# A two-layer hybrid decoder: sums of the experts back to the tokens in converted passes, one gathering product for 256 slots, another order of the parts, a later residual

## The chip, the cores and the metric

One core of a Trainium2 chip runs the whole kernel. The metric is the device time of one execution in microseconds; the time before is the median of three runs. TensorE multiplies, VectorE (DVE) and ScalarE (ACT) do the elementwise work and read the products out of PSUM, SyncE (SP) issues the weight loads, GpSimd (POOL) does little.

## The reference, cut to what matters

Two layers on 256 tokens of 1024 channels. Each has a token mixer and a channel mixer, with a layer norm behind each. The channel mixer of layer 0 is one dense SwiGLU, that of layer 1 is the part that the change touches:

```python
def moe_ffn(h, w_router, w13, w2):               # 256 tokens, 8 experts, top 2
    logits = (t @ w_router).astype(jnp.float32)
    top_v, top_i = lax.top_k(logits, TOP_K)
    probs = jax.nn.softmax(top_v, axis=-1)
    gates = (jax.nn.one_hot(top_i, N_EXPERTS) * probs[..., None]).sum(-2)
    for e in range(N_EXPERTS):
        out = out + gates[:, e, None] * swiglu(t, w13[e], w2[e])
...
x = layer_norm(ALPHA * x + (1 + g_f) * y, ln_g[l, 1], ln_b[l, 1])
```

Everything is float32, and each expert has 3584 hidden channels, so that its three matrices are 42 loads of 1 MB.

## The kernel before

**Two kinds of product.** A float32 product leaves two records in the trace and is slow. The kernel avoids it where much work goes over the same weights: `convert` (L120) rounds a half megabyte of weights to a short form, `hi` (ACT, L123), and takes the rest, `lo` (DVE, L125), and `passes` (L496) makes three fast products of `hi` and `lo` of both factors. `split` (L79) does the same for activations.

**Blocks.** Only tokens that chose an expert are computed for it. `gather` (L1077) multiplies the hidden state (`hhi`, `hlo`) with 0/1 matrices `Dm` and so brings the tokens of an expert into 128 slots (a wide block, kept as `hi` and `lo`, computed in passes on converted weights) or 64 slots (a narrow block, float32, computed straight on the loaded weights, two column halves side by side; a block of 32 slots has four). A channel group of 128 has one bank of PSUM. The products are appended to a list, `bits`, from which a "down" part takes one after each quarter of its work (`a_bit`, L1204).

**Stages of the expert layer.** From about 800 us the router runs and the seven experts with loads by register are ranked by their number of tokens. The last expert's first two steps of seven run meanwhile (L1404). In them the eight calls of the first `gather` (`first_and_last`, L1384) are made: one wide block of 128 slots for the most used expert, and one tile of 2 x 64 slots. Then `ranked` (L1420) runs the rest: here rank 0 (a wide block and a narrow one of 32 slots: "two-block" parts), rank 1 (wide), and ranks 2 to 6 (narrow, "light"). L1425 to L1436 write one order of parts by hand: a step of an expert is "up a", "up b" (2 MB of weights each; one part "up" of 4 MB in a light expert) and "down" (2 MB). Heavy parts are put between the light ones in proportion to a cost, 3 for a two-block part and 1 for another. Weight loads go through a ring of seven 1 MB buffers in the same order, as early as the buffers are free.

**Back to the tokens.** When an expert's last "down" is done, `combine` (L1230) scales its result by the gate and `g1` into a float32 tile `ys` (L1244), and appends two `add` calls (L1246) to `bits`. Each multiplies two halves of 512 channels with the 0/1 matrix `DT` (float32, L1250; for a block of 64 slots the two halves lie in the two halves of the partitions) and adds them to the residual `acc` (L1254). `acc` is made by `residual` (L397) at L1376, four VectorE operations on 128x1024, ahead of the last expert's two early steps. `last_norm` (L1262) ends the kernel.

## Time and profile before

| | us |
|---|---|
| median of 3 runs | 1743.8 (1743.49 to 1747.57) |
| the profiled execution, its own time | 1747.22 |
| its span, first to last instruction | 1745.5 |
| TensorE busy | 1670.6 (96%) |
| VectorE busy | 1017.2 (58%) |
| ScalarE busy | 719.6 (41%) |

The page cuts the span into 40 slices and gives each engine's busy share; the stretches below do the same for stages. A busy TensorE means that a product was under way, and two may overlap, so the distance between the starts of two rows is what a product costs there, not its duration. The waits tell what an engine was held up by.

### The profile page before, as it was taken

How to read it: one execution, taken by the hardware profiler on the slowest of the kernel's cores; microseconds unless marked ns; L12 is line 12 of the kernel's file. 1: busy time of each engine (PE TensorE's matmuls, PEld its weight loads, DVE VectorE, ACT ScalarE, POOL GpSimd, SP SyncE). 2: the span in 40 equal slices, each digit the busy share in tenths (PEclk: the TensorE clock that was granted, in tenths of full speed). 3: DMA queues.
4: the chain of work that ended last, by engine and by line, in shares of the span. 5: the costliest groups of instructions: out<-in, count | busy, mean ns of one | idle time of the engine just before them, and what ended most of it. 6: DMA issues, size and time to landing. Idle time of an engine off the chain costs nothing. (4 is left out here: it accounts for less than half of the span.)

```text
span 1745.5 us, 28148 instructions
## 1 busy us (share of the span) xinstructions
PE 1670.6 (96%) x11433; PEld 1276.0 (73%) x11433; DVE 1017.2 (58%) x1513; ACT 719.6 (41%) x977; POOL 39.4 (2%) x70
## 2 busy tenths in 40 slices
PE   6999999999999999998999999999999999999996
PEld 3999997999997999996766665556555555566662
DVE  2799857966667999858735633322323223545554
ACT  2764445544444855455434432122222223335440
POOL 0001000000000001000000000000000000000000
PEclk8999999999999999999899999999999999999998
DMA  9467754776664667662699999999899999999994
GB/s 394 182 247 269 264 174 154 297 262 237 224 247 186 225 265 289 243 241 97 231 400 409 416 396 364 382 397 384 354 415 361 401 386 420 380 374 418 421 420 176
DMA packets 76442, 541.19 MB, mean 310 GB/s; under 512 B 8464, under 2 KB 8720, under 8 KB 11536
## 3 DMA queue, kind: packets, MB, share of 16 engines
q1 hardware_dynamic: 74880, 534.81, 78.3%
q10 hardware_dynamic: 1424, 4.49, 0.7%
q8 instruction: 92, 1.51, 0.3%
q14 instruction: 46, 0.38, 0.1%
HBM read 538.22 MB, written 1.05 MB: 309 GB/s over the span
## 5 line engine op out<-in xcount | busy, mean ns | idle before, releaser
L125 DVE TENSOR_TENSOR lo<-raw,hi 128x1024 fp32r<-128x1024 f32 x368 | 439.4, 1220 | 148.6 <-ACT hi L123 148.3
L123 ACT CAST hi<-raw 128x1024 fp32r<-128x1024 f32 x374 | 382.0, 1048 | 254.1 <-PE grp L486 155.7
L485 PE MATMUL grp<-h_hi,hi 128*128 128x256 f32 x1408 | 402.2, 286 | 0.5 <-ACT hi L123 0.5
L487 PE MATMUL grp<-h_hi,lo 128*128 128x256 f32 x1408 | 397.8, 283 | 0.0
L486 PE MATMUL grp<-h_lo,hi 128*128 128x256 f32 x1408 | 397.5, 282 | 0.0
L485 PEld LDWEIGHTS grp<-h_hi,hi 128*128 128x128 f32 x1408 | 268.6, 191 | 3.6 <-issue 1.2
L486 PEld LDWEIGHTS grp<-h_lo,hi 128*128 128x128 f32 x1408 | 268.6, 191 | 2.0 <-issue 1.7
L487 PEld LDWEIGHTS grp<-h_hi,lo 128*128 128x128 f32 x1408 | 268.5, 191 | 0.8 <-issue 0.8
L1176 DVE TENSOR_TENSOR ss<-bank,ss 128x256 f32<-128x256 f32 (+1 forms) x42 | 16.9, 403 | 236.2 <-PE bank L1129 235.0
L499 PE MATMUL bank<-lo,x_parts 128*128 128x512 f32 x336 | 137.6, 410 | 4.7 <-DVE lo L125 4.3
L497 PE MATMUL bank<-hi,x_parts 128*128 128x512 f32 x336 | 135.4, 403 | 2.8 <-ACT hi L123 2.8
L1174 ACT ACTIVATE ss<-bank 128x256 f32<-128x256 f32 (+1 forms) x42 | 15.4, 367 | 289.0 <-PE bank L1129 289.0
L498 PE MATMUL bank<-hi,x_parts 128*128 128x512 f32 x336 | 132.3, 394 | 0.0
L1129 PE MATMUL bank<-raw,x_pairs 128*64 128x256 f32 x1056 | 122.2, 384 | 0.0
L125 DVE TENSOR_TENSOR lo<-raw_moe,hi 128x1024 fp32r<-128x1024 f32 x76 | 89.6, 1220 | 27.8 <-ACT hi L123 25.7
L1129 PEld LDWEIGHTS bank<-raw,x_pairs 128*64 128x64 f32 x1056 | 74.1, 138 | 42.0 <-issue 3.2
L497 PEld LDWEIGHTS bank<-hi,x_parts 128*128 128x128 f32 x336 | 63.2, 188 | 31.5 <-ACT hi L123 19.5
L1129 PE MATMUL bank<-raw,mg 128*64 128x512 f32 (+1 forms) x432 | 85.6, 537 | 0.5 <-ACT mg L1189 0.5
L299 DVE SCALAR_TENSOR_TENSOR acc<-raw,cond,acc 128x512 f32<-128x512 f32 x120 | 83.3, 745 | 0.0
L499 PEld LDWEIGHTS bank<-lo,x_parts 128*128 128x128 f32 x336 | 63.0, 187 | 26.9 <-DVE lo L125 10.2
L123 ACT CAST hi<-raw_moe 128x1024 fp32r<-128x1024 f32 x76 | 76.1, 1050 | 15.4 <-PE bank L498 13.4
L1189 ACT COPY mg<-bank 128x256 f32<-128x256 f32 (+1 forms) x42 | 15.0, 356 | 158.9 <-PE bank L1186 158.9
(321 smaller groups left out, 2299.1 us busy)
## 6 DMA issues: line engine op xcount, KB each, us to landing
raw<-in_moe_w_dram SPq DMA_DIRECT2D x192, 1024.0 KB, 8.6
raw_moe<-in_moe_w_dram SPq DMA_DIRECT2D x96, 1024.0 KB, 8.4
raw<-in_w_in_dram SPq DMA_DIRECT2D x68, 1024.0 KB, 4.9
raw_big<-in_moe_w_dram SPq DMA_DIRECT2D x48, 1024.0 KB, 8.5
raw<-in_w_ada_dram SPq DMA_DIRECT2D x46, 1024.0 KB, 5.1
raw<-in_dense_w_dram SPq DMA_DIRECT2D x42, 1024.0 KB, 4.8
raw<-in_w_out_dram SPq DMA_DIRECT2D x8, 1024.0 KB, 4.8
raw_start<-in_w_in_dram SPq DMA_DIRECT2D x4, 1024.0 KB, 12.3
```

Source lines behind the costliest of these rows:

```text
L123: A.copy(hi, raw)
L125: V.tensor_tensor(lo, raw, hi.bitcast(F32), op=OP.subtract)
L299: V.scalar_tensor_tensor(a, raw[:, jj], cond[:, j:j + 1], a, op0=OP.mult, op1=OP.add)
L485: T.matmul(o, whi[:, kk, fs], hi[:, k], start=first, stop=False, skip_group_check=True)
L486: T.matmul(o, whi[:, kk, fs], lo[:, k], start=False, stop=False, skip_group_check=True)
L487: T.matmul(o, wlo[:, kk, fs], hi[:, k], start=False, stop=k == KC - 1, skip_group_check=True)
L497: T.matmul(o, ahi, whi, start=start, stop=False)
L498: T.matmul(o, alo, whi, start=False, stop=False)
L499: T.matmul(o, ahi, wlo, start=False, stop=stop)
L1129: T.matmul(o[c * p:c * p + p, 0:n], act, w[:, c * n:c * n + n], start=start, stop=stop)
L1174: A.activation(dst, src, AF.Silu)
L1176: V.tensor_tensor(dst, src, dst, op=OP.mult)
```

## The change

There are four edits.

- `combine` scales into a float32 tile `ytmp`, then splits it into `hi` and `lo` (`split`, one ACT and one DVE operation); `DT` is in the converted form too, and `add` makes two fast products for each half, four in all, where it made two float32 products. A wide block's `hi` and `lo` fill both tiles of the ring `ys`, so what is left in `bits` is run down to nothing ahead of each `combine` (L1298: `bits_left(0)` for `bits_left(2)`).
- In `gather`, two blocks of different kinds are multiplied at once, 256 columns wide, for `hhi` and for `hlo`, into two places in the bank. The wide block's `hi` is copied by ACT and its `lo` by DVE; of the 2 x 64 tile ACT copies the first sum and DVE adds the second to it. Before, one engine did all copies of a channel group, the two engines by turns.
- A two-block part costs 4, not 3, in the order written by hand.
- `residual` and the tiles `ys`, `ytmp` and `x_pairs` come behind the last expert's two early steps instead of ahead of them.

```diff
--- before.py
+++ after.py
@@ -1078,25 +1078,26 @@
             n, left = len(blocks), [KC]
             Dm = places(blocks, F32R)
             pair = [narrow(pieces) for pieces in blocks]
-            runs = [slice(0, n)] if len(set(pair)) == 1 else [slice(i, i + 1) for i in range(n)]
+            together = all(pair)
 
             def channel(ch):
                 left[0] -= 1
                 pt = bank((128, 2, n, 128))
                 copy = A.copy if ch % 2 == 0 else V.tensor_copy
-                for r in runs:
-                    together = pair[r.start]
-                    for o, h in enumerate((hhi, hlo)):
-                        dst = pt[:, 0 if together else o, r].rearrange("p n s -> p (n s)")
-                        for tb in range(2):
-                            T.matmul(dst, h[:, tb, ch * 128:ch * 128 + 128], Dm[tb][:, r.start * 128:r.stop * 128],
-                                     start=tb == 0 and not (together and o), stop=tb == 1 and not (together and not o))
+                for o, h in enumerate((hhi, hlo)):
+                    dst = pt[:, 0 if together else o].rearrange("p n s -> p (n s)")
+                    for tb in range(2):
+                        T.matmul(dst, h[:, tb, ch * 128:ch * 128 + 128], Dm[tb], start=tb == 0 and not (together and o),
+                                 stop=tb == 1 and not (together and not o))
                 for i, d in enumerate(dsts):
-                    if pair[i]:
+                    if together:
                         copy(d[:, ch], pt[:, 0, i])
-                        continue
-                    for o in range(2):
-                        copy(d[o][:, ch], pt[:, o, i])
+                    elif pair[i]:
+                        A.copy(d[:, ch], pt[:, 0, i])
+                        V.tensor_tensor(d[:, ch], pt[:, 1, i], d[:, ch], op=OP.add)
+                    else:
+                        A.copy(d[0][:, ch], pt[:, 0, i])
+                        V.tensor_copy(d[1][:, ch], pt[:, 1, i])
 
             bits.extend([lambda ch=ch: channel(ch) for ch in range(KC)])
             if not spread:
@@ -1118,7 +1119,7 @@
                 T.transpose(pt[:, tb * 128:tb * 128 + 128], t, ident)
             gs = small.tile([128, 1], F32, tag="gs", bufs=4, name="gs")
             V.tensor_reduce(gs, pt[:, 0:S], axis=AX.X, op=OP.add)
-            DT = small.tile([128, S], F32, tag="DT", bufs=3, name="DT")
+            DT = small.tile([128, S], F32R, tag="DT", bufs=3, name="DT")
             V.tensor_scalar(DT, pt[:, 0:S], 0.0, None, op0=OP.is_gt)
             return gs, DT
 
@@ -1223,32 +1224,35 @@
 
             over_halves(xs, 2, wide, side)
 
-        def next_ys():
-            ys_ring.rotate(1)
-            return ys_ring[0]
+        def next_ys(n):
+            ys_ring.rotate(n)
+            return [ys_ring[i] for i in range(n)]
+
 
         def combine(b, y, gs, DT):
-            ys = next_ys()
+            side = b.tiles == 2
             n = 1024 // b.tiles
             if b.tiles == 4:
 
-                G.memset(ys, 0.0)
-            for c in range(2 if b.tiles < 4 else 4):
+                G.memset(ytmp, 0.0)
+            for c in range({1: 2, 2: 1, 4: 4}[b.tiles]):
                 cs = slice(c * 512, c * 512 + 512) if b.tiles == 1 else slice(0, n)
                 ps = slice(c * 32, c * 32 + 32) if b.tiles == 4 else slice(0, 128)
                 src = y[c] if b.tiles == 1 else y[ps, cs]
-                dst = ys[ps, c * n // 512, c * n % 512:c * n % 512 + n] if b.tiles == 4 else ys[:, c]
-                if b.tiles == 2 and c:
-                    continue
+                dst = ytmp[ps, c * n // 512, c * n % 512:c * n % 512 + n] if b.tiles == 4 else ytmp[:, c]
                 g1_ = {1: g1, 2: g1_parts[:, 0], 4: g1_parts[:, 1]}[b.tiles][ps, cs]
                 V.scalar_tensor_tensor(dst, src, gs[ps], g1_, op0=OP.mult, op1=OP.mult)
+            t = next_ys(1 if side else 2)
+            parts = (t[0][:, 0:1], t[0][:, 1:2]) if side else t
+            split(*parts, ytmp[:, 0:1] if side else ytmp)
 
             def add(tb):
                 pos_ = [bank() for _ in range(2)]
-                for hf_, po in enumerate(pos_):
-                    ps = slice(hf_ * 64, hf_ * 64 + 64) if b.tiles == 2 else slice(0, 128)
-                    T.matmul(po, DT[ps, tb * 128:tb * 128 + 128], ys[ps, 0 if b.tiles == 2 else hf_], start=True,
-                             stop=True)
+                for i, ys in enumerate(parts):
+                    for hf_, po in enumerate(pos_):
+                        ps = slice(hf_ * 64, hf_ * 64 + 64) if side else slice(0, 128)
+                        T.matmul(po, DT[ps, tb * 128:tb * 128 + 128], ys[ps, 0 if side else hf_], start=i == 0,
+                                 stop=i == 1)
                 for hf_, po in enumerate(pos_):
                     a = acc[:, tb, hf_ * 512:hf_ * 512 + 512]
                     V.tensor_tensor(a, po, a, op=OP.add)
@@ -1295,7 +1299,7 @@
                 down(ex.xs, j, ex.ys, ex.g)
                 if j == STEPS - 1:
                     for b, y, bk in zip(ex.xs, ex.ys, ex.bk):
-                        bits_left(2)
+                        bits_left(0)
                         combine(b, y, *bk)
                 return
             for b in ex.xs:
@@ -1373,7 +1377,6 @@
                     T.transpose(pt[:, cc], hf[:, q * 4 + cc, tb * 128:tb * 128 + 128], ident)
                 ds = slice(q * 512, q * 512 + 512)
                 split(hhi[:, tb, ds], hlo[:, tb, ds], pt.rearrange("p a b -> p (a b)"))
-        acc = residual(z, *gb)
         regs = [nc.values_load(ints[0:1, r:r + 1], engines=[mybir.EngineType.SP], min_val=0, max_val=last)
                 for r in range(NR)]
         w_r = [(dyn(moe_w13, r), dyn(moe_w2, r)) for r in regs]
@@ -1388,20 +1391,24 @@
 
         x_pair = h4("x_pair", F32, (128, KC, 128))
         g1_parts = h4("g1_parts", F32, (128, 2, 512))
-        ys_ring = deque(h4("ys", F32, (128, 2, 512)) for _ in range(2))
-        for t in ys_ring:
-            G.memset(t[:, 0, 0:1], 0.0)
         for i, p in ((0, 64), (1, 32)):
             for c in range(128 // p):
                 ps, n = slice(c * p, c * p + p), 8 * p
                 A.copy(g1_parts[ps, i, 0:n], g1[ps, c * n:c * n + n])
-        x_pairs = big.tile([128, 2, KC, 128], F32, tag="t8", name="x_pairs")
-        G.memset(x_pairs[:, 0, 0, 0:1], 0.0)
         x_first = []
 
         ywide = [bank() for _ in range(2)]
         e_last = Expert((units_of(moe_w13[last]), units_of(moe_w2[last])), x_last)
         run(parts_of((e_last, 0, LAST_STEPS)), {(e_last, 0): lambda: x_first.extend(first_and_last())})
+
+        acc = residual(z, *gb)
+        ys_ring = deque(h4("ys", F32R, (128, 2, 512)) for _ in range(2))
+        for t in ys_ring:
+            G.memset(t[:, 0, 0:1].bitcast(F32), 0.0)
+        ytmp = h4("ytmp", F32, (128, 2, 512))
+        G.memset(ytmp[:, 0, 0:1], 0.0)
+        x_pairs = big.tile([128, 2, KC, 128], F32, tag="t8", name="x_pairs")
+        G.memset(x_pairs[:, 0, 0, 0:1], 0.0)
 
 
         first = [(Expert(w_r[NR - 1], [], "plain"), 0, "up"), (e_last, LAST_STEPS, "up a")]
@@ -1425,7 +1432,7 @@
             heavy_ = parts_of(e7, *((e, 0, STEPS) for e in ex[:NR - narrow]))
             light_ = parts_of(*((e, 0, STEPS) for e in ex[:NR - narrow - 1:-1]))
 
-            cost = [3 if len(e.xs) == 2 else 1 for e, _, _ in heavy_]
+            cost = [4 if len(e.xs) == 2 else 1 for e, _, _ in heavy_]
             end = sum(cost) if narrow > 1 else sum(c for c, p in zip(cost, heavy_) if p[0] in (e7[0], ex[0]))
             order__, done, i = [], 0, 0
             for n, p in enumerate(light_):
```

## Rows read from the trace of the kernel before

**Rows 1.** The page: busy time of the engines (us, share of the span, instructions).
```profile
PE 1670.6 (96%) x11433; PEld 1276.0 (73%) x11433; DVE 1017.2 (58%) x1513; ACT 719.6 (41%) x977; POOL 39.4 (2%) x70
```

**Rows 2.** Busy time by stretch: the stretch in us, its length, then PE, PEld, DVE, ACT and POOL busy (instructions), granted TensorE clock, DMA share, GB/s. The first stretch is the two early steps of the last expert; the other four are the run over all experts that follows.
```profile
816.00:870.50 54.50, 48.85 (x225) 38.97 (x223) 43.05 (x72) 32.50 (x47) 0.00 (x0) 0.91 0.58 213
870.50:1017.00 146.50, 143.08 (x839) 97.47 (x840) 72.18 (x94) 59.86 (x80) 0.00 (x0) 1.00 1.00 406
1017.00:1450.00 433.00, 418.55 (x3248) 243.69 (x3244) 140.91 (x171) 108.84 (x159) 0.95 (x1) 1.00 0.95 384
1450.00:1600.00 150.00, 145.34 (x852) 89.91 (x850) 71.91 (x82) 50.92 (x64) 0.00 (x0) 1.00 0.98 394
1600.00:1716.00 116.00, 111.11 (x613) 74.08 (x614) 61.58 (x66) 49.67 (x59) 0.00 (x0) 1.00 1.01 419
```

**Rows 3.** All that TensorE's products waited for between 880 and 1725 us: waiting tile and line, the releaser, us in total, times, longest us.
```profile
PE bank L1186 <- DVE ss L1176: 13.6, 22, 0.6
PE bank L1118 <- DVE Gt L1117: 3.8, 7, 1.2
PE bank L497 <- ACT hi L123: 2.8, 2, 1.4
PE bank L497 <- ACT mg_hi L80: 2.8, 3, 1.1
PE bank L499 <- DVE lo L125: 2.6, 4, 1.4
PE bank L1250 <- DVE ys L1244: 0.9, 1, 0.9
PE bank L1186 <- DVE ms L1176: 0.8, 1, 0.8
PE bank L1129 <- ACT mg L1189: 0.5, 1, 0.5
```

**Rows 4.** What ScalarE waited for in the same stretch: the longer of the two rows that name a DMA, same columns.
```profile
ACT hi L123 <- DMA raw_moe<-in_moe_w_dram: 1.8, 3, 0.8
```

**Rows 5.** Timeline of TensorE (start us, us, line, operation, count), two places in which products of `combine` run: for a block of 128 slots at 1067, for one of 64 slots at 1228, and what follows each.
```profile
1067.15 1.98 PE L1250 MATMUL bank<-ys,DT 128*128 128x512 f32 x4
1069.07 1.94 PE L1129 MATMUL bank<-raw,mg 128*64 128x512 f32 x8
...
1228.69 1.13 PE L1250 MATMUL bank<-ys,DT 64*128 64x512 f32 x4 [0.85 <-DVE ys L1244]
1229.75 0.50 PE L497 MATMUL bank<-hi,mg_hi 128*128 128x512 f32 x1
1230.09 0.39 PE L498 MATMUL bank<-hi,mg_lo 128*128 128x512 f32 x1
1230.32 0.40 PE L497 MATMUL bank<-hi,mg_hi 128*128 128x512 f32 x1
```

**Rows 6.** Timeline of TensorE, products of `gather`: 128 columns wide at 839 us, 256 wide at 918 us.
```profile
839.58 0.39 PE L1092 MATMUL bank<-Dm,h_hi 128*128 128x128 f32 x2
839.80 0.39 PE L1092 MATMUL bank<-Dm,h_lo 128*128 128x128 f32 x2
...
917.92 0.40 PE L1092 MATMUL bank<-Dm,h_hi 128*128 128x256 f32 x2
918.16 0.40 PE L1092 MATMUL bank<-Dm,h_lo 128*128 128x256 f32 x2
```

**Rows 7.** Timeline of VectorE in the early steps of the last expert: the first and the last operation of `residual`, a row of conversions, and the low half of the activations behind them.
```profile
822.04 1.22 DVE L399 TENSOR_TENSOR xA<-z,lng 128x1024 f32<-128x1024 f32 x1
...
827.79 1.22 DVE L400 TENSOR_TENSOR xA<-xA,lnb 128x1024 f32<-128x1024 f32 x1
...
837.38 4.62 DVE L125 TENSOR_TENSOR lo<-raw,hi 128x1024 fp32r<-128x1024 f32 x4
841.92 0.68 DVE L81 TENSOR_TENSOR mg_lo<-bank,mg_hi 128x512 fp32r<-128x512 f32 x1
```

**Rows 8.** Timeline of TensorE in the same steps; in brackets its idle time before the row and the releaser.
```profile
827.93 0.50 PE L499 MATMUL bank<-lo,x_parts 128*128 128x512 f32 x1 [1.75 <-DVE lo L125]
...
838.61 0.73 PE L497 MATMUL bank<-hi,mg_hi 128*128 128x512 f32 x2 [1.43 <-DVE lo L125]
...
842.66 0.79 PE L498 MATMUL bank<-hi,mg_lo 128*128 128x512 f32 x1 [0.59 <-DVE mg_lo L81]
843.25 0.63 PE L499 MATMUL bank<-lo,mg_hi 128*128 128x512 f32 x1
...
846.66 0.63 PE L499 MATMUL bank<-lo,mg_hi 128*128 128x512 f32 x1
...
858.61 0.66 PE L1186 MATMUL bank<-ident,ms 128*128 128x128 f32 x4 [1.37 <-DVE ms L1176]
```

**Rows 9.** Groups of instructions by line and shape from 700 us on: busy us, mean ns of one, idle before and releaser.
```profile
L125 DVE TENSOR_TENSOR lo<-raw,hi 128x1024 fp32r<-128x1024 f32 x165 | 194.5, 1220 | 57.2 <-ACT hi L123 57.1
...
L80 ACT CAST mg_hi<-bank 128x512 fp32r<-128x512 f32 x21 | 12.3, 585 | 51.0 <-PE bank L1186 51.0
...
L1099 DVE CAST x_parts<-bank 128x128 fp32r<-128x128 f32 x16 | 3.9, 284 | 6.0 <-PE bank L1092 6.0
```

**Rows 10.** Timeline of VectorE at the end: the last scaling in `combine` and the first addition to the residual.
```profile
1728.11 0.75 DVE L1244 SCALAR_TENSOR_TENSOR ys<-bank,gs,g_parts 128x512 f32<-128x512 f32 x1 [5.70 <-PE bank L1129]
1730.07 0.69 DVE L1254 TENSOR_TENSOR xA<-bank,xA 128x512 f32<-128x512 f32 x1 [1.21 <-PE bank L1250]
```

## The prediction

> **What bounds the kernel now.** I read the page first: TensorE is busy for 1670.6 us, 96% of the span [rows 1]. Then the busy times by stretch, since the change touches only what lies behind 816 us. In the four stretches of the run over all experts TensorE is busy for 143.08 + 418.55 + 145.34 + 111.11 = 818.1 of 845.5 us, while the DMA share is 0.95 to 1.01, with 406, 384, 394 and 419 GB/s [rows 2]. Both look full, so the third view decides: what do the products wait for? All eight rows name VectorE or ScalarE, none a landing [rows 3], and the engine that reads the loaded weights ahead of TensorE, ScalarE, waited 1.8 us in all for the loads of its longer row [rows 4]. So TensorE is the bound from 870 us to the end of the weights, and DMA is only kept full by the ring of buffers. How far is it from being the bound? The stretches moved 406x146.5 + 384x433 + 394x150 + 419x116, that is 333 MB; at 419 GB/s this takes 796 us, 49 less than the 845.5. A gain under some 40 us is not eaten by the loads.
>
> In the early steps, 816 to 870.5 us, it is otherwise. VectorE is busy for 43.05 of 54.5 us, TensorE's clock was granted at 0.91 only [rows 2], and products stand still for 1.75, 1.43, 0.59 and 1.37 us behind VectorE; after the third the products start (846.66 - 843.25)/8 = 0.43 us apart for nine products, where 0.23 is their pace elsewhere: the lower of the two clock levels, 1.2 GHz, behind the standstill [rows 5, 8].
>
> **The sum, part by part**, against the profiled execution of 1747.22 us (span 1745.5, 1.7 outside it).
>
> Wide blocks' sums. Blocks with 128 or 32 slots use all partitions: last expert, rank 0 twice, rank 1, so 4 blocks x 2 `add` = 8. One now takes 1069.07 - 1067.15 = 1.92 us for four records [rows 5]. Afterwards it is four fast products. Their pace is 1230.32 - 1230.09 = 0.23 us, the first behind another kind costs 1230.09 - 1229.75 = 0.34 [rows 5]: 0.34 + 3x0.23 = 1.03. That saves 0.89, 7.1 in all; with 0.11 more for the change back 6.2, without either change 8.0. All eight run where TensorE is the bound. I take 7.0.
>
> Narrow blocks' sums. Five blocks, ten `add`, two of them in the tail. One takes 1229.75 - 1228.69 = 1.06 us [rows 5], little over half of a wide one with as many records: the two halves of the partitions multiply at once. For fast products the trace shows no such pair. If they pair too, two slots of 0.23 and the changes of kind make 0.57 to 0.68, saving 0.4 to 0.5; if not, 1.03 to 1.14, saving nothing or losing 0.1. Eight of them: -0.6 to +3.9. I take 3.2, since the nearest row, the same shape in float32, pairs. The Trainium skill (TensorEngine Tiling (Array Packing), Key Properties) says that tiles operate independently and that different tiles multiply in parallel; by it the term is 3.2, without it about 0. The float32 row at 1228 agrees, and no row shows it for the converted form.
>
> The first gather. 8 groups x 8 products of 128 columns at (839.80 - 839.58)/2 = 0.11 us are 7.0; 8x4 of 256 at (918.16 - 917.92)/2 = 0.12 are 3.8 [rows 6]. Saving 3.2; some of these products fill stalls, so 2 is the lower end. Against it, the copies: 24 of 128x128 become 32 operations, one more for each group on the average of the two engines, 0.28 us each [rows 9]. Hidden where the engines idle, 8x0.28 where not: I take -1.3. The later single gather (rank 1) only spreads its copies over both engines, which idle there.
>
> The residual. Its four operations stand on VectorE from 822.04 to 829.0, with conversions between, 4x1.22 = 4.9 us; behind them `lo` conversions run without a gap to 841.92, where the low half that TensorE waits for comes last [rows 7]. Without it the wait of 1.75 us goes at once: the lower end. If the queue is empty by 836, the 1.43 and the 0.59 go too, and so do the nine products at half clock, 9x0.2 = 1.8: together 5.6, the upper end. What is late next is the wait at 858.61 [rows 8], which hangs on a chain from product to SiLU to transpose and stays. I take 5.0, as 4.9 us less on the queue reach to the 836. Where it goes: behind the early steps VectorE is busy for 72.18 of 146.5 us [rows 2], which hides 4.9 us; without that cover it would cost 4.9. `acc` is not read before the first sums, those at 1067 [rows 5]. The two one-column memsets and the tiles move with it on POOL, which is idle, and no DMA moves.
>
> The split in `combine`. ACT and DVE get one more operation each for a block: 0.59 and 0.68 us for a narrow one, as conversions of the same size take [rows 7, 9], for a wide one 1.22 on VectorE [rows 9] and by the same proportion 1.05 on ScalarE. Throughput is there, but the sums come 1.3 or 2.3 us later. Queued behind a waiting sum are the next products of TensorE. Mostly a light "up" lies between. It does not for rank 4, whose sums now fall into the two-block "down" that follows its last part, nor for rank 0, where the emptied `bits` put the first block's sums straight behind its own split: up to 2x0.75 for scaling [rows 10] and 2.3. Ends 0 and -6, I take -1.5.
>
> The tail. From the start of the last scaling to the first addition it is 1.96 us [rows 10]. The split puts 1.3 us between, the shorter products give some 0.4 back: -0.9, ends -0.6 and -1.4.
>
> The order. Walking the loop by hand, the 21 two-block parts lie between 23 light "up" parts where they lay between 21, and other heavy parts come three or four at a time instead of three. TensorE does the same products with the same neighbours in another order, and it is not fed too late [rows 3]. I take 0. Of more pieces in a row, the conversions still keep up: four halves a part cost VectorE 4x1.22 = 4.9 us [rows 9] against 24 products x 0.23 = 5.6.
>
> Sum: 7.0 + 3.2 + 3.2 - 1.3 + 5.0 - 1.5 - 0.9 = 14.7 us. From 1747.2 that gives 1732.5; the median of the runs is 3.4 lower, so I forecast 1743.8 - 14.7 = **1729**.
>
> **The rivals.**
>
> The two engines take turns on one bank. The new copies of a channel group go ACT, DVE, ACT, DVE out of one bank of PSUM. If each waits for the one before, and stands behind a conversion of 1.22 us [rows 9], ScalarE is held for up to 8x2x1.22 = 19.5 us in the stretch in which it makes the `hi` halves. Before, one engine read a whole group, so no row shows it; against it stands that ScalarE idles for 22 of the 54.5 us [rows 2]. Price: the early steps lose their 6.9, and if that idle time covers a third, 13 of the 19.5 are left, with 7.8 gained later: 1743.8 - 7.8 + 13 = 1749. It turns slower than before from 7.8 us of uncovered hold on, half a microsecond for each of 16 waits. The Trainium skill (PSUM — Partial Sum Buffer, "PSUM bank collisions raise a hardware error") states that the compiler puts a dependency between any two instructions of different engines on one bank, reads of ACT and DVE too: by it the turns are taken. No row of this trace shows it. Chance 0.10, of which 0.05 at or above 1749.
>
> The sums stand in TensorE's way. If the later operands are exposed for all blocks, 4x3.8 and 4x2.0 = 23 us are lost less what the light "up" hides. With 14 exposed it is 1743, no change. For it: one such wait of 0.9 exists, in the row of L1250 [rows 3]; against: it is only one. Chance 0.12.
>
> The order pays by itself. If the full DMA did bound the stretches at 1.00 and the two-block stretch alone were bound by TensorE, levelling them would be worth up to the shortfall there, (419 - 384)/419 x 433 = 36 us, of which the spread over 23 instead of 21 gives about a third: 1718. Against it are rows 3 and 4. Chance 0.10.
>
> The residual is not moved in effect, because VectorE still waits for the same `hi` halves: the gain there falls to 1.75, 1732. This is inside the forecast's own range.
>
> **How the numbers follow.** The forecast has 0.68, with its own range of 1724 to 1739: all upper ends together are 1724, and all lower ends 1744, and two bounds that are far apart, the pairs and the wait for the split, are not both at their lower end as a rule. What a measurement of this kernel can tell from no change is 0.3%, 5.2 us. Faster (below 1738.6): 0.65 of the forecast, 0.10 of the order, 0.01 of the exposed sums, 0.01 of the turns: 0.77. Slower (above 1749): 0.05 of the turns and 0.02 of the exposed sums: 0.07. The same: 0.16. The range that leaves out 2 in 10 takes in the order at one end and most of the exposed sums at the other: 1717 to 1743.
>
> **What would show it.** The first light product should start at about 863 to 865 instead of 870.5, with the 1.75 us wait gone and VectorE's queue empty at 837. Each group of four sums should span 1.0 (wide) and 0.6 (narrow). DMA's GB/s should rise in the two-block stretch just as TensorE gets faster, and products should still not wait for a landing. Wrong would be: a wait of ACT on DVE within the gather's copies, a wait on `ys` above 1 us for several blocks, or an order that shifts TensorE's idle time by more than 3 us.

## The result and the profile after

The kernel after takes 1732.25 us (median of 4 runs, 1728.52 to 1733.71), the kernel before on the same chips 1745.57 (4 runs): ratio 0.9923, 95% interval 0.9911 to 0.9935, 13.3 us less. The forecast was 14.7 less and 1729. The total came out right by luck, since errors in its terms cancelled: the experiments show that the converted sums, the largest gain in the forecast, gave nothing, and that the order, put at nothing, is worth 4.4 us alone and 9.7 beside the converted sums.

The profiled execution of after took 1728.52 us (span 1726.8), 3.7 below its median, and that of before 1747.22, 1.7 above its own, so profile against profile overstates the gain. What lies ahead of the last expert's early steps, where no edit changes a product, lasts 814.7 to 819.0 us in the fourteen traces. So I use traces for places and stretches, and medians for totals.

The page's engine line, then the windows, which answer to [rows 2] (from, to, length, busy time of PE, PEld, DVE, ACT, POOL, granted clock, DMA share, GB/s; 870.5 is now inside the later run, since the early steps end at 858.65):

```profile
PE 1652.2 (96%) x11401; PEld 1270.8 (74%) x11401; DVE 1026.0 (59%) x1526; ACT 727.9 (42%) x990; POOL 39.7 (2%) x71
```

```profile
816.00:870.50 54.50, 51.51 (x276) 40.55 (x275) 48.68 (x90) 35.34 (x53) 0.23 (x3) 1.00 0.75 285
1017.00:1450.00 433.00, 415.99 (x3234) 240.43 (x3232) 132.59 (x167) 101.87 (x153) 0.00 (x0) 1.00 0.97 394
```

The share of TensorE is 96% as before: 18 us less work in 18 us less time. In the early steps the clock is 1.00 where it was 0.91. GB/s rose in the two-block stretch from 384 to 394. The forecast tied this to a faster TensorE, but it comes with the order: the order alone (below) has 393, the converted sums alone 381 (1017 to 1450 us in each trace). The row of the order alone:

```profile
1017.00:1450.00 433.00, 418.48 (x3246) 240.63 (x3237) 130.13 (x165) 100.08 (x152) 0.96 (x1) 1.00 0.97 393
```

TensorE's waits behind the early steps, 875 to 1708 us (who waits <- for what: total, times, longest; answers to [rows 3]; rows left out):

```profile
PE bank L1187 <- DVE ss L1177: 13.3, 22, 0.6
PE bank L497 <- ACT hi L123: 7.6, 6, 2.5
PE bank L1254 <- ACT ys L80: 1.2, 2, 1.0
```

The row on `hi` was 2.8 and is 7.6. That is the row that grew, and the next section follows it. Timeline rows of after, products of TensorE (start, duration, engine, line, out<-in, count): the early steps' waits and their end (answers to [rows 8]), a narrow and a wide sum, each with the product that follows it, and the tail's (answers to [rows 5, 10]):

```profile
835.41 0.73 PE L497 MATMUL bank<-hi,mg_hi 128*128 128x512 f32 x2 [1.44 <-ACT mg_hi L80]
850.35 0.66 PE L1187 MATMUL bank<-ident,ms 128*128 128x128 f32 x4 [1.55 <-DVE ms L1177]
858.65 1.08 PE L1130 MATMUL bank<-raw,x_pair 128*64 128x256 f32 x8
1078.91 0.73 PE L1254 MATMUL bank<-ys,DT 64*128 64x512 f32 x4
1079.58 1.08 PE L1130 MATMUL bank<-raw,mg 128*64 128x512 f32 x4
1501.79 1.19 PE L1254 MATMUL bank<-ys,DT 128*128 128x512 f32 x4
1502.91 1.08 PE L1130 MATMUL bank<-raw_big,mg 128*64 128x512 f32 x4
1710.21 1.46 PE L1254 MATMUL bank<-ys,DT 64*128 64x512 f32 x8 [1.53 <-ACT ys L80]
```

From its start to the next product, a narrow sum of four fast products takes 0.67 where a wide one takes 1.12: the halves pair in the converted form too. VectorE's queue in the early steps (answers to [rows 7]) reads the low halves without the residual between them, which now stands at 859.89:

```profile
832.61 4.62 DVE L125 TENSOR_TENSOR lo<-raw,hi 128x1024 fp32r<-128x1024 f32 x4
837.15 0.68 DVE L81 TENSOR_TENSOR mg_lo<-bank,mg_hi 128x512 fp32r<-128x512 f32 x1
859.89 1.22 DVE L399 TENSOR_TENSOR xA<-z,lng 128x1024 f32<-128x1024 f32 x1
```

### The profile page after: what moved, and what is told of

The parts are those of the page before. It is cut to its first block, busy times and chain, and to the rows that moved or that the text cites. A ratio compares the mean times of both kernels' runs of the same rounds, so it can differ in the third digit from the quotient of the medians.

```text
span 1726.8 us, 28133 instructions
## 1 busy us (share of the span) xinstructions
PE 1652.2 (96%) x11401; PEld 1270.8 (74%) x11401; DVE 1026.0 (59%) x1526; ACT 727.9 (42%) x990; POOL 39.7 (2%) x71
## 5 line engine op out<-in xcount | busy, mean ns | idle before, releaser
L1177 DVE TENSOR_TENSOR ss<-bank,ss 128x256 f32<-128x256 f32 (+1 forms) x42 | 16.9, 402 | 181.2 <-PE bank L1130 181.2
L125 DVE TENSOR_TENSOR lo<-raw_moe,hi 128x1024 fp32r<-128x1024 f32 x80 | 93.9, 1220 | 29.1 <-ACT hi L123 28.9
L1130 PE MATMUL bank<-raw,x_pairs 128*64 128x256 f32 x928 | 107.4, 382 | 0.1
L1130 PE MATMUL bank<-raw,mg 128*64 128x512 f32 (+1 forms) x528 | 106.5, 548 | 0.5 <-ACT mg L1190 0.5
L1130 PEld LDWEIGHTS bank<-raw,x_pairs 128*64 128x64 f32 x928 | 64.6, 137 | 36.1 <-issue 2.5
```

Source lines behind the costliest of these rows:

```text
L125: V.tensor_tensor(lo, raw, hi.bitcast(F32), op=OP.subtract)
L1130: T.matmul(o[c * p:c * p + p, 0:n], act, w[:, c * n:c * n + n], start=start, stop=stop)
L1177: V.tensor_tensor(dst, src, dst, op=OP.mult)
```

## The experiments

Three stretches are read from every trace: the early steps (first product of the last expert's first step to the first light product), the run (to the last record of the last light "down"), and the tail (to the end). "At half clock" is the time that the clock took: over stretches of 4 us, length x (1 - granted clock). Each ratio is to the runs of before that were timed beside that kernel (their medians are 1744.9 to 1745.6).

| kernel | median us (runs) | ratio to before | early | run | tail |
|---|---|---|---|---|---|
| before | 1745.4 (21) | | 53.78 | 856.93 | 18.06 |
| after | 1732.25 (4) | 0.9923 [0.9911, 0.9935] | 42.15 | 849.44 | 18.71 |
| before + order | 1741.0 (11) | 0.9975 [0.9966, 0.9984] | 53.76 | 852.33 | 18.09 |
| before + residual later | 1739.94 (5) | 0.9964 [0.9951, 0.9978] | 47.50 | 857.16 | 18.15 |
| before + gather | 1742.5 (11) | 0.9985 [0.9976, 0.9994] | 47.23 | 857.15 | 18.08 |
| before + converted sums | 1753.41 (5) | 1.0046 [1.0032, 1.0060] | 50.74 | 861.42 | 18.68 |
| after, order undone | 1741.98 (11) | 0.9983 [0.9974, 0.9991] | 42.16 | 862.85 | 18.66 |
| after, sums undone | 1728.1 (4) | 0.9901 [0.9887, 0.9915] | 42.15 | 849.56 | 18.08 |
| before + sums, split on VectorE | 1750.24 (12) | 1.0021 [1.0008, 1.0034] | 54.68 | 858.69 | 18.46 |
| after, split on VectorE | 1729.81 (6) | 0.9906 [0.9888, 0.9924] | 42.16 | 853.02 | 18.54 |
| after, split on GpSimd | 1737.88 (5) | 0.9954 [0.9941, 0.9966] | 42.12 | 857.87 | 19.42 |
| after, split given out later | 1734.51 (5) | 0.9945 [0.9932, 0.9959] | 42.13 | 851.94 | 18.70 |
| after, sums undone, light transposes held | 1746.92 (11) | 1.0006 [0.9997, 1.0015] | 42.14 | 867.45 | 18.09 |
| after, split on GpSimd, transposes held | 1751.16 (6) | 1.0036 [1.0024, 1.0048] | 42.14 | 869.07 | 19.44 |

**Each part alone.** The order:

```diff
-            cost = [3 if len(e.xs) == 2 else 1 for e, _, _ in heavy_]
+            cost = [4 if len(e.xs) == 2 else 1 for e, _, _ in heavy_]
```

> The kernel before with only the cost of a two-block part raised from 3 to 4, so that the 21 two-block parts stand between 23 light parts instead of 21; sums, gather and residual as before. Theory of the parts (the order moves the same products and is worth nothing): within 2 us of before, stretch from the first light product to the last light down product still 856.9 us. Rival, the order pays by itself: 8 to 12 us faster, and that stretch 845 to 849 us. Third case, the order alone does harm that the other parts hide: over 3 us slower, with new waits of TensorE on ScalarE's hi halves.

4.4 us faster, between the two. Its trace shows where: TensorE's waits from 872 to 1728 us (left out: rows under 0.9 and those unchanged) are

```profile
PE bank L1250 <- DVE ys L1244: 1.9, 2, 1.0
PE bank L497 <- ACT hi L123: 1.4, 1, 1.4
PE bank L499 <- DVE lo L125: 0.9, 2, 0.5
```

against 2.8 on `hi`, 2.8 on `mg_hi` (now 0.7) and 2.6 on `lo` before. Ahead of the tail (whose wait of 0.9 is in the first row) all rows of the view add up to 22.4 us where before has 27.8; half clock in the run is 3.4 for 1.7. Together that is 3.7 of the 4.6 by which the run is shorter: the same products among other neighbours wait less. None of its waits is for a landing, as in before [rows 3].

The residual, with the tiles allocated behind it:

```diff
-        acc = residual(z, *gb)
...
         run(parts_of((e_last, 0, LAST_STEPS)), {(e_last, 0): lambda: x_first.extend(first_and_last())})
+        acc = residual(z, *gb)
```

> The kernel before with only the residual (and with it the two tiles of scaled outputs and the tile of the narrow blocks' gathered columns) allocated and traced behind the early steps. Theory of the parts: the VectorE queue is shorter by 4.9 us there, the wait of 1.75 us goes, the first light product moves from 870.5 to 865.5 (864.9 to 868.8) and the whole is 5 us faster, all behind it unchanged. Rival, the early steps need both edits: under 2 us faster, with the first light product at 868.5 or later, because the products of the gather still fill the place. Second rival, the residual alone makes the measured gain of the early steps: first light product at 859 to 861, 10 to 12 us faster.

5.4 us faster, and the early steps 6.3 shorter, the run and the tail unchanged: the theory of the parts.

The gather, by its new `channel` alone:

```diff
-                for r in runs:
-                    together = pair[r.start]
-                    for o, h in enumerate((hhi, hlo)):
...
+                for o, h in enumerate((hhi, hlo)):
+                    dst = pt[:, 0 if together else o].rearrange("p n s -> p (n s)")
```

> The kernel before with only the new gather (one product for 256 slots, copies from both engines); the residual stays early. Theory of the parts: 32 products of 256 columns in place of 64 of 128 save 2 to 3.2 us, the extra copies cost 0 to 2.2, so the whole is 1 to 2.5 us faster and the first light product starts at about 868.5. Rival, the two engines take turns on one bank: ScalarE waits on VectorE in the gather copies by some 0.5 us each and the whole is 3 us slower or more. Second rival, the early steps' measured gain comes from here: first light product at 861 or earlier, 8 us faster or more.

2.9 us faster, a little over the 1 to 2.5 of the parts. Its early steps are 6.55 shorter in the trace, far more than the 3.2 that the products save. The two engines do take turns on a bank. In the later gather of after, where VectorE mostly idles, its copy starts 0.03 us behind the end of ScalarE's copy out of the same bank, and the trace names that copy as releaser at seven of eight places (ScalarE's copy, then VectorE's):

```profile
1186.11 0.27 ACT L1099 CAST x_parts<-bank 128x128 fp32r<-128x128 f32 x1 [2.05 <-PE bank L1090]
1186.41 0.29 DVE L1100 CAST x_parts<-bank 128x128 fp32r<-128x128 f32 x1 [0.46 <-ACT x_parts L1099]
```

But a turn costs the length of a copy, not that of a conversion as the rival had it, and in the early steps of after an engine waits for the other within the copies only twice, 0.2 us each. What goes besides the products is half clock, for windows of before in the early steps (same columns as above) show it twice:

```profile
840.00:844.00 4.00, 3.40 (x15) 3.03 (x15) 3.20 (x6) 0.60 (x3) 0.00 (x0) 0.54 0.96 371
844.00:848.00 4.00, 4.00 (x12) 3.08 (x12) 1.25 (x2) 2.09 (x2) 0.00 (x0) 0.60 0.44 160
860.00:864.00 4.00, 4.00 (x13) 3.18 (x14) 1.29 (x2) 1.56 (x4) 0.00 (x0) 0.60 0.52 221
```

That is 4 x (0.46 + 0.40 + 0.40) = 5.0 us. With the residual alone or the gather alone 1.7 is left, and none in any of the eight traces that have both. But the converted sums alone, with neither edit, have none either, though TensorE waits for 6.8 us in their early steps. So one trace of each does not show which edit keeps the clock up, and the median's 2.9 is no more than the products give.

The sums, with `combine`, the converted mask and the emptied bits:

```diff
-            DT = small.tile([128, S], F32, tag="DT", bufs=3, name="DT")
+            DT = small.tile([128, S], F32R, tag="DT", bufs=3, name="DT")
...
+            split(*parts, ytmp[:, 0:1] if side else ytmp)
...
-                        bits_left(2)
+                        bits_left(0)
```

> The kernel before with only the sums in two converted passes (scaled output split, mask converted, gathered bits emptied ahead of each scaling); order, gather and residual as before. Theory of the parts: 8 wide sums of 1.92 become 1.03 to 1.13, 8 narrow ones of 1.06 become 0.57 to 0.68, less 1.5 for exposed splits and 0.9 in the tail: 7 to 8 us faster, tail 0.7 to 0.9 longer, early steps unchanged at 870.5. Rival, exposed splits eat it: under 3 us faster, with waits of TensorE on the split of over 5 us in all or on hi conversions queued behind it.

8 us slower: the rival's side and beyond it. The trace explains 2 of the 8, for its execution took 1747.38, 6 less than the median: the run is 4.5 and the tail 0.6 longer, and the early steps are 3.0 shorter, with their products in another order and at full clock. In the run, 9.8 us more of waits and 3.4 more at half clock stand against some 9.6 of shorter products. Where the other 6 us go no trace shows. The place of the waits it does show. Behind the light "down" (ends 1374.4), on all three engines:

```profile
1370.77 3.65 PE L1129 MATMUL bank<-raw,mg 128*64 128x512 f32 x16
1370.88 0.37 ACT L1189 COPY mg<-bank 128x256 f32<-128x256 f32 x1 [4.07 <-PE bank L1186]
1374.50 0.75 DVE L1243 SCALAR_TENSOR_TENSOR ytmp<-bank,gs,g_parts 128x512 f32<-128x512 f32 x1 [4.16 <-PE bank L1129]
1375.28 0.62 ACT L80 CAST ys<-ytmp 128x512 fp32r<-128x512 f32 x1 [4.03 <-DVE ytmp L1243]
1375.81 1.99 ACT L123 CAST hi<-raw 128x1024 fp32r<-128x1024 f32 x2
1376.90 0.50 PE L497 MATMUL bank<-hi,x_parts 128*128 128x512 f32 x1 [2.48 <-ACT hi L123]
1379.92 0.63 PE L498 MATMUL bank<-hi,x_parts 128*128 128x512 f32 x1
1380.35 0.63 PE L499 MATMUL bank<-lo,x_parts 128*128 128x512 f32 x1
```

ScalarE is free from 1371.2, but the split's cast (L80) is next in its queue and waits 4.03 us for the scaling, which waits for the "down". The `hi` conversions of the next heavy part stand behind the cast, so TensorE stands for 2.48 us; then its products start 0.43 apart instead of 0.23, the lower of its two clocks. In before, at the same place, the conversions follow the copy at once, during the "down", and the product waits for nothing:

```profile
1376.76 0.37 ACT L1189 COPY mg<-bank 128x256 f32<-128x256 f32 x1 [4.07 <-PE bank L1186]
1377.03 1.99 ACT L123 CAST hi<-raw 128x1024 fp32r<-128x1024 f32 x2
```

There are three such waits in this trace (1069.67, 1376.90, 1543.02), and `hi` waits come to 12.0 us.

**In the company of the other parts.** The order undone in after:

```diff
-            cost = [4 if len(e.xs) == 2 else 1 for e, _, _ in heavy_]
+            cost = [3 if len(e.xs) == 2 else 1 for e, _, _ in heavy_]
```

> The kernel after with the cost of a two-block part put back from 4 to 3, all else as after. Theory that the order shelters the sums (alone, the converted sums made the kernel 8 us slower, by ScalarE's cast of the scaled outputs standing ahead of the hi conversions; only the new spacing moves that cast out of the way): 1742 to 1747 us, with two or three waits of 2.48 us of TensorE on hi conversions at about 1060, 1365 and 1530 where after has one. Rival, the order is worth only what it is worth alone and the sums were harmed alone by the early residual: 1735 to 1738 us, with one such wait.

9.7 us slower than after (1742, the theory's lower end), with the three waits of 2.48 (1062.36, 1371.15, 1537.20). The order is worth 4.4 alone and 9.7 here, as it leaves one of the three. In after, rank 4's own sums follow the scaling at the second place (they wait 0.98), and at the third the conversions stand ahead of the cast (at 1507.66, the cast at 1509.56; the wait is 1.41). The waits without the order come to 39.1 us against 30.2, half clock in the run to 6.8 against 1.7: together 14.0, and the run is 13.4 longer.

Only the sums put back to float32, and the late residual kept:

```diff
-            split(*parts, ytmp[:, 0:1] if side else ytmp)
...
-            DT = small.tile([128, S], F32R, tag="DT", bufs=3, name="DT")
+            DT = small.tile([128, S], F32, tag="DT", bufs=3, name="DT")
...
-                        bits_left(0)
+                        bits_left(2)
```

> The kernel after with the sums in float32 as before (one product a half, no split, two gathered bits left ahead of a scaling); order, gather and late residual as after. Theory of the on-record sum (converted sums save 8.7 us of products and lose 1.5 and 0.9): 1738 to 1741 us, first to last light product 856 to 858 us. Rival, the casts' waits give it all back even in the new order: 1731 to 1734 us, no different from after. Adding the four edits measured alone gives 1732.7.

1728.1, below every run of after, and 3 us below the rival's range, too, which had the sums give nothing. The stretch of the run is equal in the two traces (849.56, 849.44). So the theory of the on-record sum has fallen: in this kernel the converted sums give nothing, and by the medians they cost 4 us, which is at the edge of what the runs can tell (the intervals of the two ratios overlap by 0.0004). Its waits:

```profile
PE bank L1251 <- DVE ys L1245: 1.9, 2, 1.0
PE bank L497 <- ACT hi L123: 1.4, 1, 1.4
PE bank L499 <- DVE lo L125: 0.9, 2, 0.5
```

`hi` 1.4 against 7.6. It beats before clearly and after by its median, which is the lowest of all kernels here.

**Whose queue?** The cast on VectorE, alone on before and in after:

```diff
-            split(*parts, ytmp[:, 0:1] if side else ytmp)
+            src = ytmp[:, 0:1] if side else ytmp
+            V.tensor_copy(parts[0], src)
+            V.tensor_tensor(parts[1], src, parts[0].bitcast(F32), op=OP.subtract)
```

> The converted sums alone on the kernel before, with the high half of the scaled outputs rounded by VectorE instead of ScalarE, so that no operation on ScalarE waits for the scaling. Theory of ScalarE's queue: the three waits of 2.48 us on hi conversions go, and the products at half clock behind each with them, hi waits in all fall from 12.0 to 3 to 5 us, and the kernel is 8 to 13 us faster than with the cast on ScalarE, 1738 to 1745 us, so no slower than before. Rival, the loss lies in the sums' later operands or in the emptied queue of gathered bits: within 3 us of 1753.

> The kernel after with the high half of the scaled outputs rounded by VectorE instead of ScalarE. Theory of ScalarE's queue: the one wait of 2.48 us at 1062 goes, with some 1.2 us at half clock behind it, 2 to 5 us faster than after: 1727 to 1730 us; tail as after or 0.2 longer. Rival, VectorE's own queue (lo conversions stand behind one operation more) takes the place of it: 1732 to 1735 us, with new waits of TensorE on lo.

1750.24 and 1729.81, only 3.2 and 2.4 better, and neither is clear of the noise (the intervals of the ratios touch or overlap). So the first misses its theory, which had 8 to 13, and the second lies in its theory's range without telling it from no change. The `hi` waits of 2.48 are gone, as the theory said, but it forgot the other queue: on before, the waits on `lo` rise from 1.4 with the cast on ScalarE to 6.9, the longest 2.5. One place of it (before + sums, split on VectorE):

```profile
1381.04 0.75 DVE L1243 SCALAR_TENSOR_TENSOR ytmp<-bank,gs,g_parts 128x512 f32<-128x512 f32 x1 [4.16 <-PE bank L1129]
1381.83 0.43 DVE L1247 CAST ys<-ytmp 128x512 fp32r<-128x512 f32 x1
1382.29 0.69 DVE L1248 TENSOR_TENSOR ys<-ytmp,ys 128x512 fp32r<-128x512 f32 x1
1382.90 2.35 DVE L125 TENSOR_TENSOR lo<-raw,hi 128x1024 fp32r<-128x1024 f32 x2
1384.17 0.50 PE L499 MATMUL bank<-lo,x_parts 128*128 128x512 f32 x1 [1.77 <-DVE lo L125]
```

Now the `lo` conversion stands behind three operations instead of one, and TensorE waits 1.77 for it where before waited 0.57. So I kept out of both queues and put both operations on GpSimd:

```diff
-            split(*parts, ytmp[:, 0:1] if side else ytmp)
+            src = ytmp[:, 0:1] if side else ytmp
+            G.tensor_copy(parts[0], src)
+            G.tensor_tensor(parts[1], src, parts[0].bitcast(F32), op=OP.subtract)
```

> The kernel after with both operations of the split of the scaled outputs on GpSimd, which is idle there, so that neither ScalarE's nor VectorE's queue holds an operation that waits for it. Theory of the queues (the converted sums save some 8.5 us of products, and the waits and half-clock stretches behind the split's place in the two queues take it back): no wait of TensorE above 1 us on hi or lo at 1062, as with float32 sums, hi waits fall from 7.6 to 1.4 to 4 us, and the time is 1722 to 1727 us, faster than after and than after with float32 sums (1728.1). Against it: GpSimd's two operations take some us, so the sums' own operands come later; rank 0's and rank 4's sums and the tail may lose 1 to 4 us each. Rival, the loss sits in the sums themselves (the shorter products bring TensorE back to the same later waits): 1730 to 1734 us with the waits on hi and lo gone.

1737.88, outside both ranges: the wait at 1062 went, and others came, of the kind that the expectation had named, though its ranges left no room for them. At rank 4, whose sums stand right behind, GpSimd took 1.53 us for the cast, with VectorE's `lo` conversions running beside it. In the eight places of the two GpSimd traces where VectorE did nothing beside it, as in the first row, the same cast took 0.61:

```profile
1216.35 0.61 POOL L1248 CAST ys<-ytmp 128x512 fp32r<-128x512 f32 x1 [149.19 <-DVE ytmp L1244]
1359.10 1.53 POOL L1248 CAST ys<-ytmp 128x512 fp32r<-128x512 f32 x1 [140.79 <-DVE ytmp L1244]
1360.69 0.49 PE L1256 MATMUL bank<-ys,DT 64*128 64x512 f32 x2 [2.00 <-POOL ys L1248]
1360.72 2.12 POOL L1249 TENSOR_TENSOR ys<-ytmp,ys 128x512 fp32r<-128x512 f32 x1
1362.89 0.79 PE L1256 MATMUL bank<-ys,DT 64*128 64x512 f32 x1 [1.70 <-POOL ys L1249]
```

Waits on `ys` are 7.6 us in all. Last, I left the split on its old engines but gave it out one light part later, as the first of the block's bits, its cast pinned behind what was traced on ScalarE by then:

```diff
-            split(*parts, ytmp[:, 0:1] if side else ytmp)
...
+            def halves_of():
+                src = ytmp[:, 0:1] if side else ytmp
+                tc.keep_in_program_order(A.copy(parts[0], src))
+                V.tensor_tensor(parts[1], src, parts[0].bitcast(F32), op=OP.subtract)
+            bits.append(halves_of)
```

> The kernel after with the split of the scaled outputs taken out of the scaling step and given out as the first of the block's bits of work, so that it is queued a light part later, behind the conversions issued by then, with its operands long ready; still ScalarE and VectorE, still four converted products a sum. Theory of the queues: the 2.48 us wait on hi at 1062 and the wait on ys at 1357 go, the sums keep their 8.5 us, and the time is 1722 to 1728 us, at or under after with float32 sums (1728.1). Rival, the converted sums can't pay here because each block's three extra operations find another place ahead of a conversion or of a sum: 1730 to 1735 us, with waits of the same total at other places.

1734.51, the rival's range. The 2.48 at 1062 is gone and `hi` waits are 3.7, but where rank 0's sums must follow at once, the pinned cast stands behind conversions that wait for a landing:

```profile
1498.19 1.99 ACT L123 CAST hi<-raw 128x1024 fp32r<-128x1024 f32 x2 [14.32 <-DMA raw<-in_moe_w_dram]
1500.09 1.04 ACT L1261 CAST ys<-ytmp 128x1024 fp32r<-128x1024 f32 x1
1501.18 2.07 PE L1253 MATMUL bank<-ys,DT 128*128 128x512 f32 x4 [4.45 <-ACT ys L1261]
```

**The largest wait left.** The 22 waits of 0.6 on `ss` look like 13 us to be had: the transposes of a light part follow its very last product. I held them behind the light "down" that was traced ahead of them, and gave the gate tile two buffers:

```diff
-                    T.transpose(pt[:, cc], s_[:, cc * 128:cc * 128 + 128], ident)
+                    t = T.transpose(pt[:, cc], s_[:, cc * 128:cc * 128 + 128], ident)
+                    if b.lo is None and cc == 0:
+                        tc.keep_in_program_order(t)
...
-                t = small.tile([128, 128], F32, tag="Gt", bufs=1, name="Gt")
+                t = small.tile([128, 128], F32, tag="Gt", bufs=2, name="Gt")
```

> The kernel after with float32 sums, the light blocks' transposes held behind the products traced ahead of them (so they no longer follow the very up whose activations they read), and two buffers for the gate tile whose second transpose waits for the first. Theory (the 22 waits of 0.6 us on ss and 7 on Gt, 13.7 and 3.8 us, stand on the path): both go, 12 to 17 us faster than 1728, 1711 to 1716 us. Rival, the freed place is taken by the next wait, ScalarE's copy of the turned columns now standing ahead of hi conversions: 1722 to 1730 us.

> The kernel after with the split on GpSimd, and with the light transposes held back and two gate tiles. If the theories of the queues and of the light waits both hold: 1707 to 1713 us. If the split on GpSimd is late for the sums: 1714 to 1720 us. Rival, the waits of the light parts only move: 1720 to 1728 us.

1746.92 and 1751.16: 18.8 and 13.3 slower than without it. All waits on `ss` are gone, and this took their place (float32 sums, waits, then one place):

```profile
PE bank L497 <- ACT hi L123: 30.9, 24, 1.6
```

```profile
1111.94 0.44 PE L1187 MATMUL bank<-ident,ss 128*128 128x128 f32 x2
1112.42 0.37 ACT L1192 COPY mg<-bank 128x256 f32<-128x256 f32 x1 [6.86 <-PE bank L1187]
1112.69 2.00 ACT L123 CAST hi<-raw_moe 128x1024 fp32r<-128x1024 f32 x2
1113.79 0.50 PE L497 MATMUL bank<-hi,x_parts 128*128 128x512 f32 x1 [1.41 <-ACT hi L123]
```

Here it is the copy of the turned columns that holds the conversions, until the "down" ends: 1.3 on the average of 24 places (1.41 at this one) instead of 0.6. It is the rival of that expectation, larger than I had put it, and the clearest evidence for the queue: an operation that has nothing to do with the sums, moved in the same way, makes a wait of the same kind.

## Why the prediction was right, point by point

- **Wide and narrow sums' products**, 7.0 and 3.2: the step was right. From its start to the next product, as in [rows 5], a wide sum fell from 1.92 to 1.12, a narrow one from 1.06 to 0.67, the pair that the float32 row promised: 8 x 0.80 + 8 x 0.40 = 9.6, an estimate from sums that wait for nothing.
- **The split exposed**, 1.5 with ends 0 and 6: this step failed, in place and in size. What I asked, who waits for the sums, came out small: waits on `ys` in the run are 1.5 us, 1.0 with float32 sums. But I counted ScalarE's operation as throughput; what stands behind the cast in ScalarE's queue was not asked, though the trace of before shows `hi` conversions made during the light "down" (the two rows at 1376 above). Measured in after, against float32 sums: 6.2 us more waiting ahead of the tail on `hi`, `ys` and `lo` (9.5 for 3.3), 1.7 at half clock, no shorter run; by the medians the whole edit costs 4 us where 7.8 were forecast as gain. By the medians the size is that of the rival "the sums stand in TensorE's way" (some 14 us exposed); the time was not its 1743 (1741.6, if its 14 take the place of the 1.5), since the order and the early steps covered it. The edit also empties `bits` ahead of each scaling; no run changes that alone.
- **The early steps**, 3.2 - 1.3 + 5.0 = 6.9: mechanism right in the main, sizes off. They are 11.6 shorter in the trace: 5.0 at half clock (I had 1.8, the second stretch at 860 was left out), 2.4 of waits (5.4 to 3.0 in all), 3.2 of gather products, 10.6 in all; the extra copies cost nothing that shows. The waits of 1.75 and 0.59 went, but that of 1.43 stayed (1.44 at 835.41): VectorE's queue was out of its way, and ScalarE's `mg_hi` ended it instead. The wait at 858 stayed as forecast, at 850.
- **The order**, 0: this step failed. "The same products with the same neighbours" was wrong: the neighbours of a heavy part decide whether its first conversions are in time. It is worth 4.4 alone and 9.7 with the converted sums, and shifts TensorE's waits by 5.4 and 8.9 us, where the prediction's own sign of being wrong was 3. The rival "pays by itself" had the sign, but 26 us of gain and another mechanism: TensorE waits for no landing in either order.
- **The tail**, -0.9: measured -0.65.
- **The rival of the two engines on one bank**: the turns are taken, as it said, but each is short, and its 13 us did not come.

So a forecast within 3.3 us came from +11.6 for 6.9 and +9.7 for 0, against about -4 for +7.8: errors that cancelled, and so luck. (The three do not add up to 13.3, since 9.7 holds what the order spares the converted sums, and 11.6 is read from one trace.) The alone-gains add up to 4.4 + 5.4 + 2.9 - 8.0 = 4.7 of the 13.3; of the other 8.6 the order's shelter for the sums is 5.3 (9.7 less 4.4). The three other edits together give 16.9 by the medians where alone they give 12.7. The traces show part of this: over the three stretches they give 19.0 together and 16.9 as a sum of alone ones. The run with all three has no half clock, where the order alone has 3.4, and is 2.8 shorter; the early steps give back 1.2, since the residual and the gather alone each count some of the same half clock. What the timed executions do beyond that stays open; their mean clock is higher (median 0.9905, order alone 0.987), but they have no trace to show where.

## What to carry to other kernels

An operation added to an engine that also feeds the bound engine is priced by what stands behind it in that engine's queue and by what it waits for, not by its duration alone: ask of each one "what is next in line, and who is due for it?". A wait taken off the bound engine comes back if the freed operation is queued ahead of the next feed; look at the queue before moving it. Undo each part from the final kernel as well as adding it to the old one: a part that looks free in the total can be carried by another.

## What the runs showed of the hardware

- Time follows the mean granted clock from one execution to the next: the split on VectorE alone took 1744.0 us at 0.989 and 1753.5 at 0.983, and before 1742.8 at 0.991 and 1747.4 at 0.987. So medians of few runs can differ by more than one trace shows. The number of standstills does not settle it: the converted sums alone have more than before (37.5 us of waits in the run for 27.7) and a lower clock (median 0.985 for 0.989), but the order alone has fewer (22.4) and a lower one, too (0.987). In the stretch ahead of the early steps, in which no edit changes a product, half clock takes 6.8 us in the trace where it is shortest, 814.7 us, and 13.7 where it is longest, 819.0.
- The length of a standstill does not tell whether the clock falls. In after, behind 2.48 us at 1062.48 it stays up; behind 0.98 at 1357.16 it falls to its lower level for part of the last two stretches shown here, and so it does in the converted sums alone behind the same 2.48 us at 1069.67 (granted 0.81 and 0.76 from 1068 to 1076):

```profile
1064.00:1068.00 4.00, 4.00 (x30) 2.95 (x31) 3.09 (x3) 1.28 (x2) 0.00 (x0) 1.00 0.96 399
1356.00:1360.00 4.00, 2.79 (x10) 1.31 (x9) 3.06 (x4) 3.51 (x5) 0.00 (x0) 0.87 1.01 424
1360.00:1364.00 4.00, 4.00 (x13) 2.43 (x13) 3.93 (x6) 0.90 (x1) 0.00 (x0) 0.70 1.00 422
```

- Copies by ScalarE and VectorE out of one bank went one behind the other, 0.03 us from the end of one to the start of the next (1186.38 and 1186.41 in after), where two copies by one engine start 0.16 us apart in before (840.23 and 840.39).
- GpSimd took 0.61 us for a cast of 128x512 where VectorE took 0.43 and ScalarE 0.62, and 1.53 in the two places where `lo` conversions of VectorE ran beside it; that they are the cause no run shows.
